# Modulation blocks one per tile in the gate and pointwise stages; the heads' token sums in an up-projection bank

## The chip, the cores and the metric

The kernel runs on one core of a Trainium2 chip. The metric is device time in microseconds from the start of the program to its end; the median of several runs is compared. The core has five engines that run side by side, each with its own instruction queue that is worked off strictly in order: TensorE (matrix products, PE in the profile, its weight loads PEld), VectorE (DVE), ScalarE (ACT), GpSimd (POOL) and SyncE (SP), which here issues every DMA. SBUF is the on-chip memory, PSUM the eight banks into which TensorE writes.

## What is computed

Two layers of a decoder trunk on 512 tokens of width 2048, in float32. Cut to what matters here:

```python
for l in range(2):
    mod = silu(c) @ ada_w[l] + ada_b[l]                 # (2048) @ (2048, 6144)
    shift, scale, gate = split(mod, 3)
    h = rms_norm(x, norm_g[l]) * (1 + scale) + shift
    z = h @ w_in[l]
    q_lat, kv_lat, k_rope, mla_gate, conv_in, conv_gate = split(z)
    # group B: 8 heads of latent attention, q and k RMS-normed per head (sums of squares per token)
    mla_out = attention(q_lat, kv_lat, k_rope) * silu(mla_gate)
    # group A: GLU, causal depthwise convolution (31 taps), LayerNorm, swish, pointwise product
    u = silu(layer_norm(conv31(glu(conv_in)))) @ w_pw[l] + b_pw[l]
    conv_out = u * silu(conv_gate)
    x = x + gate * (concat(mla_out, conv_out) @ w_out[l])
```

## The kernel before

Everything stands with channels on the 128 partitions and the 512 tokens along the row, so a tile is 128 x 512. Each large product runs in three passes (`mm3`, L248): weights and activations are split into a rounded part (hi) and a rest (lo), and hi x hi, hi x lo and lo x hi are added up in one PSUM bank. A weight chunk of 8 x 128 x 128 (512 KB) is loaded into one of four `raw` buffers by SP (`load_w`, L228), copied to hi by ScalarE (L242) and its rest taken by GpSimd, or by VectorE in layer 1's pointwise and output products (L243). `Stream` (L253) puts these steps in order: one step is four chunks of 128 channels, twelve matmuls.

The order on each queue is laid down when the program is built, by a planner that takes the instructions in the order of the source and lets a later one go first where its inputs and buffers are free. `tc.issue_after(ins)` adds an edge: instructions inside it come after `ins` on the engine of `ins` in that order. It adds no wait on the chip, and it does not touch instructions on other engines.

The stages of a layer are: the input products; eight heads of attention (`attend`, L735), between which the remaining input products are filled in (`fill`); then the **gate stage** (L905 to L930: eight tiles `cg`, the products of the convolution gate), the **pointwise stage** (L953 to L963: eight tiles `pw`, product with `w_pw`) and the **output projection** (L970 to L1017: sixteen tiles `wo`, 48 matmuls each). Beside the gate stage runs the LayerNorm of the convolution's result, as pieces in a queue `bgq` with a cost each; `bg(VBUD)` after each step takes pieces out until 1.5 is spent: the last convolution taps (`conv_ops`), two empty pieces, `ln_mean`, eight `ln_center`, two empty, the token sums of `vacc`, two empty, the spread of the result (`rsqrt_bc`), eight `ln_silu`. Their results are split into `u2`, which the pointwise product reads. `cat_split` (L939) splits the sixteen tiles of the concatenation for the output projection.

The modulation is computed in **blocks**: `Gemv.block` (L332) loads 128 rows of `ada_w` transposed, 1 MiB, into one of two `ada` buffers (SP, L335), and VectorE multiplies it by silu(c) and sums along the row in one instruction (L336). The list `todo` holds 64 blocks: 16 gates of layer 0, 32 scales and shifts of layer 1, 16 gates of layer 1. `more(n)` (L910) takes n blocks, fractions adding up. In layer 0's trailing stages 34 of them are done, in layer 1's 16. Before the change all stand in the output projection: `rate` blocks per tile, 34.5/15 and 16.5/15, each behind the instruction `behind`, which is the last split of the concatenation for the first tile and then the residual L1013 of the tile before. L1013 adds gate times the tile to x; its result is stored by SP (L1014), and the x of a tile is loaded by SP (L977).

`token_sums` (L188) sums a tile over its channels for each token, by eight or so one- or two-column matmuls into a PSUM bank of tag `pz`. That tag has one bank (L104); the transposes of the probabilities (`turn`, L741), `token_bc` and `ln_mean` use it too. The tag `up` has two, used by `up_head`, `up_values` and `values` in the heads. In the heads the sums of the next head are taken in `between` (L857), after the transposes of block 1, from F, which GpSimd adds up (L689, L690); `factors` (L694) reads them on VectorE (L701, L702).

Of the kernel before, what the change touches and what calls it, by code (L numbers as in the profile page):

```python
# [13 lines left out]
ALU = mybir.AluOpType  # L14
AX = mybir.AxisListType

P = 128
# [33 lines left out]
def hybrid_trunk(ctx, tc, xT, c, pos, invf, vec, adaT, w_s, w_t, w_kr, w_q, w_kv, w_pw, w_o, outT):  # L51
    nc = tc.nc
    V, A, T = nc.vector, nc.scalar, nc.tensor
# [52 lines left out]
    def psum(tag, n):  # L106
        return pp.tile([P, S], F32, tag=tag, bufs=NB[tag], name=nm(n))
# [77 lines left out]
        if scaled:  # L185
            V.tensor_scalar(out=y, in0=y, scalar1=RSCALE, scalar2=None, op0=ALU.mult)

    def token_sums(sq, rhs=None):  # L188

        ps, nt = psum("pz", "st"), sq.shape[1] // P  # L190
        rhs = ones[0:sq.shape[0], 0:1] if rhs is None else rhs
        w = rhs.shape[1]
        for i in range(nt):
            T.matmul(out=ps[:, i * w:(i + 1) * w], lhsT=sq[:, i * P:(i + 1) * P], rhs=rhs, start=True, stop=True)
        return ps[:, 0:nt] if w == 1 else ps[:, 0:nt * w].rearrange("p (i w) -> p i w", w=w)
# [101 lines left out]
    def bg(budget):  # L297
        while bgq and budget > 0:
            cost, fn = bgq.pop(0)
            fn()  # L300
            budget -= cost
# [43 lines left out]
    def gate(l, j):  # L345
        return mods[l][:, 32 + j:33 + j]
# [41 lines left out]
    def layer(l, xs, rstd, rpsum):  # L388
# [192 lines left out]
        for n in range(6):  # L581
            z = first[n]
# [111 lines left out]
        def factors(hd, st):  # L694

            e = hd % 2
            pst = lp.tile([P, 3, NT, 2], F32, tag="pst", name=nm("pst"))
            ms_, y, t = (pst[:, q] for q in range(3))

            b2 = lambda a: a.unsqueeze(2)  # L700
            V.tensor_mul(out=ms_[:, :, 0:1], in0=st[:, :, e:e + 1], in1=b2(rlat2[:, 1]))  # L701
            V.tensor_mul(out=ms_[:, :, 1:2], in0=st[:, :, 1 - e:2 - e], in1=b2(rlat2[:, 0]))  # L702
            V.tensor_add(out=ms_[:, :, 0:1], in0=ms_[:, :, 0:1], in1=b2(krs))
            V.tensor_scalar(out=ms_, in0=ms_, scalar1=1.0 / QKD, scalar2=EPS, op0=ALU.mult, op1=ALU.add)
            rsqrt_small(ms_, y, t)
            sc = lp.tile([P, NT], F32, tag="sc", name=nm("sc"))
            V.scalar_tensor_tensor(out=sc, in0=y[:, :, 1], scalar=SCALE, in1=rlat[:, 0], op0=ALU.mult, op1=ALU.mult)

            kft = lp.tile([P, NT], F32, tag="kft", name=nm("kft"))
            V.tensor_mul(out=kft, in0=y[:, :, 0], in1=rlat[:, 1])  # L710
            nc.sync.dma_start(out=kfd[l * H + hd], in_=kft)
            kf = ap.tile([P, S], F32, tag="kf", bufs=2, name=nm("kf"))
            nc.sync.dma_start(out=kf, in_=kfd[l * H + hd].rearrange("t i -> (t i)").partition_broadcast(P))
            return kf.rearrange("p (t i) -> p i t", i=NT), sc
# [128 lines left out]
            A.copy(out=RK[p0:p0 + 64, 0], in_=kr[0:64])  # L843
            V.tensor_sub(out=RK[p0:p0 + 64, 1 + p0 // 64], in0=kr[0:64], in1=f(RK[0:64, 0]))
        fill(1)
        fac = factors(0, token_sums(F, halves))
        conv_ops(0)
        fill(FA)
        for hd in range(H):
            fill(FB)  # L850
            if hd < H - 1:
                nxt = up_head(hd + 1)
            fill(FC)
            F = nxt[3]() if hd < H - 1 else None
            nfac = []

            def between():  # L857
                if hd < H - 1:
                    nfac.extend(factors(hd + 1, token_sums(F, halves)))
            pt = attend(hd % 2, *cur[:3], *fac, between)  # L860
            if hd % 2 == 0:
                vv_ = up_values(hd // 2)
            else:
                fill(FE)
            values(hd, pt, *vv_)
            cur, fac = nxt, nfac
# [4 lines left out]
        bp = phase.enter_context(tc.tile_pool(name=f"bp{l}", bufs=1))  # L871
        use_tmp(bp, 2)
        mean, vacc, crs = ms("mean"), ms("vacc"), ms("crs")
        ctile = []

        def ln_mean():
            pm = psum("pz", "pm")
# [3 lines left out]
        def ln_center(j):  # L881
            if j % 2 == 0:
                t = bp.tile([P, 2, S], F32, tag="c", bufs=4, name=nm("c"))
                nc.sync.dma_start(out=t, in_=cd[j // 2])
                ctile.extend((t[:, 0], t[:, 1]))
            V.tensor_sub(out=ctile[j], in0=ctile[j], in1=mean)
            square_sum(vacc, ctile[j], j)

        def ln_silu(j):
            V.tensor_mul(out=ctile[j], in0=ctile[j], in1=crs)  # L890
            A.activation(out=ctile[j], in_=ctile[j], func=AF.Silu, scale=vt("lng", j), bias=vt("lnb", j))

        bgq.extend((1.6, lambda: None) for _ in range(LAG))
# [31 lines left out]
        for j in range(NCC):  # L925
            for _ in range(4):
                ws.step()
                bg(VBUD)
        bg(1e9)
        cg = [t[:, e] for t in cg for e in range(2)]  # L930
        u2 = []
# [23 lines left out]
        for j in range(NCC):  # L955
            ws.step()
            ws.step()
            if j < 6:

                t = bp.tile([P, 2, S], F32R, tag="c", bufs=4, name=nm("cat")) if j < 4 else None  # L960
                cat[j] = cat_split(mout[j], t)
        for j in (6, 7):
            cat[j] = cat_split(mout[j])  # L963

# [8 lines left out]
        for j in range(KC):  # L973
# [36 lines left out]
                t = tp[:, j % 2]  # L1010
            else:
                t = ms("x1")
            behind = V.scalar_tensor_tensor(out=t, in0=z, scalar=gate(l, j), in1=xr, op0=ALU.mult, op1=ALU.add)  # L1013
            nc.sync.dma_start(out=outT[j] if last else x1d[j], in_=t)  # L1014
            if not last:
                nxs.append(t)
# [85 lines left out]
```

## Time and profile before

| | us |
|---|---|
| median of three runs | 1679.31 |
| lowest, highest | 1675.61, 1680.39 |
| the profiled execution | 1681.96 |
| its span, first to last instruction | 1680.2 |

The profile shows one execution. A row of grouped instructions gives engine, operation, output and inputs, their count, busy time and mean duration; a window row gives the busy time of each engine in a stretch, the clock granted to TensorE (1.00 is 2.4 GHz, 0.50 is 1.2 GHz), the busy share of the sixteen DMA engines and what they moved; the chain of waits follows the work that ended last back through what released it.

### The profile page before, as it was taken

How to read it: one execution, taken by the hardware profiler on the slowest of the kernel's cores; microseconds unless marked ns; L12 is line 12 of the kernel's file. 1: busy time of each engine (PE TensorE's matmuls, PEld its weight loads, DVE VectorE, ACT ScalarE, POOL GpSimd, SP SyncE). 2: the span in 40 equal slices, each digit the busy share in tenths (PEclk: the TensorE clock that was granted, in tenths of full speed). 3: DMA queues.
4: the chain of work that ended last, by engine and by line, in shares of the span. 5: the costliest groups of instructions: out<-in, count | busy, mean ns of one | idle time of the engine just before them, and what ended most of it. 6: DMA issues, size and time to landing. Idle time of an engine off the chain costs nothing.

```text
span 1680.2 us, 20681 instructions
## 1 busy us (share of the span) xinstructions
PE 1587.6 (94%) x7350; PEld 1299.3 (77%) x7350; DVE 1211.6 (72%) x2008; ACT 687.5 (41%) x1284; POOL 640.5 (38%) x440
## 2 busy tenths in 40 slices
PE   4988999999999999998899899999999999999999
PEld 2766778887878888877678678888787878888888
DVE  8898897888899645665469856677887786555553
ACT  4222455554544345321223355544544443532221
POOL 3565633424233445554535546243343326200000
PEclk9999999999999999999999999999999999999999
DMA  8878323222232732797885633233223335337672
GB/s 299 281 282 290 132 86 97 68 84 82 76 108 84 238 100 89 254 331 268 307 293 181 267 97 104 72 98 97 75 71 97 105 128 181 93 110 253 237 261 88
DMA packets 82890, 271.53 MB, mean 162 GB/s; under 512 B 10721, under 2 KB 21729, under 8 KB 70241
## 3 DMA queue, kind: packets, MB, share of 16 engines
q1 hardware_dynamic: 82786, 270.20, 47.5%
q8 instruction: 58, 0.95, 0.2%
q14 instruction: 46, 0.38, 0.1%
HBM read 257.55 MB, written 12.62 MB: 161 GB/s over the span
## 4 chain that ended last, share of the span: by engine, by line
PE 55%; DVE 27%; DMA 6%; ACT 6%; issue 3%; POOL 1%; SPq 0%; POOLq 0%; DVEq 0%; ACTq 0%
DVE ada L336 7%; DVE cv L547 7%; PE wo L251 4%; PE z L251 4%; PE z L249 4%; PE z L250 4%; PE wo L249 4%; PE wo L250 4%; PE cg L251 3%; PE cg L249 3%; PE cg L250 3%; DMA ada<-in_adaT_dram 3%; DMA raw<-in_w_o_dram 3%; PE pw L250 2%; PE pw L251 2%
## 5 line engine op out<-in xcount | busy, mean ns | idle before, releaser
L243 POOL TENSOR_TENSOR lo<-raw,hi 128x512 fp32r<-128x512 f32 x380 | 575.6, 1530 | 690.1 <-ACT hi L242 680.9
L242 ACT CAST hi<-raw 128x512 fp32r<-128x512 f32 (+1 forms) x512 | 306.4, 612 | 559.3 <-PE wo L250 152.9
L547 DVE SCALAR_TENSOR_TENSOR cv<-u,lvec,cv 128x512 f32<-128x512 f32 x464 | 348.7, 751 | 7.2
L249 PE MATMUL z<-h,hi 128*128 128x512 f32 (+1 forms) x782 | 308.2, 399 | 17.0 <-ACT h L357 10.9
L251 PE MATMUL z<-h,lo 128*128 128x512 f32 (+1 forms) x782 | 308.7, 395 | 8.6 <-POOL lo L243 8.5
L250 PE MATMUL z<-h,hi 128*128 128x512 f32 (+1 forms) x782 | 307.2, 393 | 0.7 <-DVE h L358 0.7
L336 DVE CUSTOM_DVE_ANT_0 ada<-ada,cb,avec 128x2048 f32<-128x2048 f32 x96 | 251.2, 2618 | 27.3 <-DMA ada<-in_adaT_dram 27.3
L249 PE MATMUL wo<-cat,hi 128*128 128x512 f32 (+1 forms) x544 | 207.8, 382 | 11.0 <-ACT hi L242 10.9
L251 PE MATMUL wo<-cat,lo 128*128 128x512 f32 (+1 forms) x544 | 207.9, 382 | 4.2 <-POOL lo L243 3.8
L250 PE MATMUL wo<-cat,hi 128*128 128x512 f32 (+1 forms) x544 | 207.0, 381 | 0.0
L249 PEld LDWEIGHTS z<-h,hi 128*128 128x128 f32 x782 | 150.0, 193 | 49.2 <-ACT h L357 13.4
L251 PEld LDWEIGHTS z<-h,lo 128*128 128x128 f32 x782 | 149.9, 192 | 43.3 <-POOL lo L243 13.5
L250 PEld LDWEIGHTS z<-h,hi 128*128 128x128 f32 x782 | 149.8, 192 | 29.5 <-DVE h L358 1.8
L243 DVE TENSOR_TENSOR lo<-raw,hi 128x512 fp32r<-128x512 f32 (+1 forms) x132 | 85.5, 660 | 80.3 <-ACT hi L242 80.1
L249 PEld LDWEIGHTS wo<-cat,hi 128*128 128x128 f32 x544 | 103.8, 191 | 32.0 <-ACT hi L242 13.1
L251 PEld LDWEIGHTS wo<-cat,lo 128*128 128x128 f32 x544 | 103.6, 190 | 26.3 <-POOL lo L243 6.8
L250 PEld LDWEIGHTS wo<-cat,hi 128*128 128x128 f32 x544 | 103.8, 191 | 19.0
L249 PE MATMUL cg<-h,hi 128*128 128x512 f32 x256 | 101.0, 394 | 0.0
L251 PE MATMUL cg<-h,lo 128*128 128x512 f32 x256 | 99.8, 390 | 0.0
L250 PE MATMUL cg<-h,hi 128*128 128x512 f32 x256 | 99.8, 390 | 0.0
L780 ACT ACTIVATE pr<-pr,smx,sc 128x128 f32<-128x128 f32 (+1 forms) x64 | 41.9, 654 | 110.3 <-DVE smx L779 110.2
L251 PE MATMUL mg<-h,lo 128*128 128x512 f32 x192 | 76.3, 397 | 2.3 <-POOL lo L243 2.3
(265 smaller groups left out, 2469.4 us busy)
## 6 DMA issues: line engine op xcount, KB each, us to landing
ada<-in_adaT_dram SPq DMA_DIRECT2D x96, 1024.0 KB, 5.5
raw<-in_w_t_dram SPq DMA_DIRECT2D x120, 512.0 KB, 3.9
raw<-in_w_o_dram SPq DMA_DIRECT2D x64, 512.0 KB, 5.8
raw<-in_w_s_dram SPq DMA_DIRECT2D x32, 512.0 KB, 6.4
raw<-in_w_pw_dram SPq DMA_DIRECT2D x16, 512.0 KB, 3.6
raw<-in_w_q_dram SPq DMA_DIRECT2D x24, 256.0 KB, 2.7
x<-in_xT_dram SPq DMA_DIRECT2D x8, 512.0 KB, 7.3
kf<-kfd SPq DMA_DIRECT2D x16, 256.0 KB, 3.9
```

Of the source, the lines that this page charges most:

```text
L242: A.copy(out=hiv, in_=rawv)
L243: i = eng.tensor_tensor(out=lov, in0=rawv, in1=f(hiv), op=ALU.subtract)
L249: T.matmul(out=ps, lhsT=whi, rhs=mhi, start=start, stop=False)
L250: T.matmul(out=ps, lhsT=whi, rhs=mlo, start=False, stop=False)
L251: T.matmul(out=ps, lhsT=wlo, rhs=mhi, start=False, stop=stop)
L336: V.tensor_tensor_reduce(out=t, in0=t, in1=self.cb, scale=1.0, scalar=vv(l, "ada_b", b), op0=ALU.mult, op1=ALU.add, accum_out=mods[l][:, b ...
L547: V.scalar_tensor_tensor(out=box[-1], in0=u[:, k:k + S], scalar=w, in1=box[0], op0=ALU.mult, op1=ALU.add)
L780: A.activation(out=pr[:, :n], in_=pr[:, :n], func=AF.Exp, scale=scl, bias=nb, accum_out=sums)
```

## The change

`token_sums` gets the bank's tag as an argument, and the heads' sums (not the latents', the rope key's or the LayerNorm's) use `up` in place of `pz`. `more(1)` is called after each of the eight gate tiles, behind the last `ln_center` or `ln_silu` instruction on VectorE and only once there is one, and after each of the first six pointwise tiles, behind the last split of the concatenation so far. In the output projection `behind` stays the last split of the concatenation, and `rate` is worked out from the blocks that are left.

```diff
         if scaled:
             V.tensor_scalar(out=y, in0=y, scalar1=RSCALE, scalar2=None, op0=ALU.mult)
-    def token_sums(sq, rhs=None):
-
-        ps, nt = psum("pz", "st"), sq.shape[1] // P
+    def token_sums(sq, rhs=None, tag="pz"):
+
+        ps, nt = psum(tag, "st"), sq.shape[1] // P
         rhs = ones[0:sq.shape[0], 0:1] if rhs is None else rhs
         w = rhs.shape[1]
         for i in range(nt):
@@ -843,7 +843,7 @@
             A.copy(out=RK[p0:p0 + 64, 0], in_=kr[0:64])
             V.tensor_sub(out=RK[p0:p0 + 64, 1 + p0 // 64], in0=kr[0:64], in1=f(RK[0:64, 0]))
         fill(1)
-        fac = factors(0, token_sums(F, halves))
+        fac = factors(0, token_sums(F, halves, "up"))
         conv_ops(0)
         fill(FA)
         for hd in range(H):
@@ -856,7 +856,7 @@
             def between():
                 if hd < H - 1:
-                    nfac.extend(factors(hd + 1, token_sums(F, halves)))
+                    nfac.extend(factors(hd + 1, token_sums(F, halves, "up")))
             pt = attend(hd % 2, *cur[:3], *fac, between)
             if hd % 2 == 0:
                 vv_ = up_values(hd // 2)
@@ -871,7 +871,7 @@
         bp = phase.enter_context(tc.tile_pool(name=f"bp{l}", bufs=1))
         use_tmp(bp, 2)
         mean, vacc, crs = ms("mean"), ms("vacc"), ms("crs")
-        ctile = []
+        ctile, ln_ins = [], [None]
         def ln_mean():
             pm = psum("pz", "pm")
@@ -883,11 +883,11 @@
                 t = bp.tile([P, 2, S], F32, tag="c", bufs=4, name=nm("c"))
                 nc.sync.dma_start(out=t, in_=cd[j // 2])
                 ctile.extend((t[:, 0], t[:, 1]))
-            V.tensor_sub(out=ctile[j], in0=ctile[j], in1=mean)
+            ln_ins[0] = V.tensor_sub(out=ctile[j], in0=ctile[j], in1=mean)
             square_sum(vacc, ctile[j], j)
         def ln_silu(j):
-            V.tensor_mul(out=ctile[j], in0=ctile[j], in1=crs)
+            ln_ins[0] = V.tensor_mul(out=ctile[j], in0=ctile[j], in1=crs)
             A.activation(out=ctile[j], in_=ctile[j], func=AF.Silu, scale=vt("lng", j), bias=vt("lnb", j))
         bgq.extend((1.6, lambda: None) for _ in range(LAG))
@@ -926,6 +926,9 @@
             for _ in range(4):
                 ws.step()
                 bg(VBUD)
+            if ln_ins[0] is not None:
+                with tc.issue_after(ln_ins[0].ins):
+                    more(1)
         bg(1e9)
         cg = [t[:, e] for t in cg for e in range(2)]
         u2 = []
@@ -959,6 +962,8 @@
                 t = bp.tile([P, 2, S], F32R, tag="c", bufs=4, name=nm("cat")) if j < 4 else None
                 cat[j] = cat_split(mout[j], t)
+                with tc.issue_after(cat_ins[0].ins):
+                    more(1)
         for j in (6, 7):
             cat[j] = cat_split(mout[j])
@@ -1010,7 +1015,7 @@
                 t = tp[:, j % 2]
             else:
                 t = ms("x1")
-            behind = V.scalar_tensor_tensor(out=t, in0=z, scalar=gate(l, j), in1=xr, op0=ALU.mult, op1=ALU.add)
+            V.scalar_tensor_tensor(out=t, in0=z, scalar=gate(l, j), in1=xr, op0=ALU.mult, op1=ALU.add)
             nc.sync.dma_start(out=outT[j] if last else x1d[j], in_=t)
             if not last:
                 nxs.append(t)
```

## Rows read from the trace of the kernel before

**Rows 1.** The page, busy time (share of the span) and count by engine.
```profile
PE 1587.6 (94%) x7350; PEld 1299.3 (77%) x7350; DVE 1211.6 (72%) x2008; ACT 687.5 (41%) x1284; POOL 640.5 (38%) x440
```
**Rows 2.** Windows by stage: window, length, busy and count by engine, clock, DMA share, GB/s.
```profile
545.00:640.00 95.00, 94.83 (x424) 78.02 (x424) 52.91 (x79) 42.33 (x69) 40.09 (x30) 1.00 0.45 150
640.00:680.00 40.00, 40.00 (x178) 33.08 (x177) 20.42 (x21) 17.46 (x31) 25.76 (x19) 1.00 0.37 114
690.00:866.00 176.00, 160.86 (x673) 128.89 (x671) 105.92 (x94) 39.49 (x68) 88.64 (x52) 0.96 0.85 307
1514.00:1666.00 152.00, 152.00 (x675) 126.00 (x674) 80.36 (x100) 34.38 (x55) 0.00 (x0) 1.00 0.63 224
```
**Rows 3.** The tile `wo`, its residual lines: count, min/median/max ns, first and last start.
```profile
L1013 DVE SCALAR_TENSOR_TENSOR x<-wo,mod,xr x15: 740/750/752, 689.9 to 866.5; 128x512 f32<-128x512 f32 x15
L1013 DVE SCALAR_TENSOR_TENSOR xr<-wo,mod,xr x15: 750/750/752, 1513.2 to 1665.6; 128x512 f32<-128x512 f32 x15
```
**Rows 4.** Windows cut at layer 0's L1013, three of them.
```profile
743.90:759.90 16.00, 13.08 (x49) 9.99 (x48) 8.50 (x8) 2.91 (x5) 7.40 (x4) 0.89 0.86 306
...
799.20:818.00 18.80, 14.35 (x49) 10.58 (x48) 6.28 (x6) 2.91 (x5) 6.76 (x6) 0.82 0.91 347
...
828.90:841.30 12.40, 11.20 (x49) 8.94 (x49) 5.90 (x7) 2.92 (x5) 6.44 (x4) 1.00 0.97 350
```
**Rows 5.** The chain that ended last, layer 0's output projection: start, length, what.
```profile
788.95 0.82 DVE ada L336
...
791.33 0.33 SPq L335
791.75 5.59 DMA raw<-in_w_o_dram
...
811.31 0.43 PE wo L249
```
**Rows 6.** SP's queue in layer 0's output projection: start, length, instruction, output and input.
```profile
677.75 0.33 SPq L232 DMA_DIRECT2D raw<-in_w_o_dram  x1
...
715.45 4.29 SPq L335 DMA_DIRECT2D ada<-in_adaT_dram  x2
...
736.08 4.97 SPq L335 DMA_DIRECT2D ada<-in_adaT_dram  x2
...
777.79 0.57 SPq L232 DMA_DIRECT2D raw<-in_w_o_dram  x1
...
789.06 0.33 SPq L1014 DMA_DIRECT2D x1d<-x  x1
```
**Rows 7.** The tile `ada`: durations in ns, and time from issue to landing.
```profile
L336 DVE CUSTOM_DVE_ANT_0 ada<-ada,cb,avec x96: 2339/2346/3404, 23.7 to 1655.4; 128x2048 f32<-128x2048 f32 x96
...
DMA to landing us min/median/max: 4.8/5.5/12.2
```
**Rows 8.** VectorE in layer 0's gate stage, in order of time; idle before and releaser in brackets.
```profile
597.95 2.68 DVE L886 TENSOR_TENSOR c<-c,mean 128x512 f32<-128x512 f32 x4 [25.50 <-ACT mean L879]
...
607.56 4.28 DVE L370 TENSOR_TENSOR vacc<-vacc,sq 128x512 f32<-128x512 f32 x3
...
617.15 0.16 DVE L215 TENSOR_SCALAR sm<-st 128x4 f32<-128x4 f32 x1 [5.31 <-PE st L194]
...
626.99 5.06 DVE L890 TENSOR_TENSOR c<-c,crs 128x512 f32<-128x512 f32 x8 [6.70 <-ACT crs L222]
...
634.18 5.15 DVE L935 TENSOR_TENSOR u<-c,u 128x512 fp32r<-128x512 f32 x8 [2.13 <-ACT u L934]
```
**Rows 9.** TensorE's waits, heads of layer 0, then of layer 1: total, times, longest.
```profile
PE st L194 <- DVE pt L751: 5.2, 5, 1.9
...
PE st L194 <- DVE pt L751: 2.7, 4, 1.1
```
**Rows 10.** GpSimd in order of time, the last step of one head's F.
```profile
299.30 1.29 POOL L690 TENSOR_TENSOR F<-F,rsq 64x512 f32<-64x512 f32 x1
```
**Rows 11.** The chain that ended last, that head's token sums.
```profile
309.04 1.05 PE st L194 x8
```

## Prediction

> **What bounds the kernel now.** I read the page first. TensorE is busy for 94% of the span [rows 1], so time is won only where it starves or runs slow. The stage windows, next, say where. Layer 1's output projection (the `wo` loop) runs without an idle moment at clock 1.00. Layer 0's, the same arithmetic, shows 160.9 us busy in 176 at clock 0.96, with the DMA engines at 307 GB/s instead of 224 [rows 2]. The gate stage and the pointwise stage of layer 0 have full TensorE and only 150 and 114 GB/s [rows 2]. The residual line L1013 puts a number on it: from first to last of 15 tiles it takes 1665.6 - 1513.2 = 152.4 us in layer 1, 10.89 us a tile, and 866.5 - 689.9 = 176.6 us in layer 0, 12.61 a tile [rows 3]. The difference, **24.2 us**, is all that can be won there.
>
> The windows cut at L1013 show how it is lost: in lumps, tiles of 16.0 and 18.8 us, whose clock is 0.89 and 0.82 [rows 4]. The chain of waits names the loop [rows 5]: a modulation block on VectorE, held behind tile 8's L1013, ends; SP then issues the next block's load, which needed that buffer; only then does SP issue the `w_o` load behind it, 5.59 us to land. TensorE waits for that, and then its matmuls stand 0.43 us apart (the 1.2 GHz level), against 10.89/48 = 0.227 in layer 1. In SP's own order, six `w_o` loads are out by 677.75, four more than tile 0 needs; when tile 8's store goes out at 789.06 only twenty are, the last at 777.79: tile 9's own two and none ahead [rows 6]. So SP's in-order queue, filled with 1 MiB block loads, is the bound there; the bytes are the reason. A tile moves 1 MiB of weights and 0.25 + 0.25 MiB of x, 1.573 MB; 34 blocks over 15 tiles are 2.3 a tile, 2.38 MB more. At 10.89 us that is 363 GB/s; the best tile reaches 350 [rows 4].
>
> **Moved blocks, layer 0.** `more(1)` behind a gate tile runs only once `ln_ins` is set. Stepped through by hand, the queue enters the stage with 49 pieces of convolution at 0.6, three a step, so 17 steps; then two empty pieces, the mean in step 19, the centres from step 20, the last step of tile 4. The trace agrees: VectorE idles 25.5 us with the convolution done and starts the centres at 597.95, late in the stage [rows 8]. Tiles 4 to 7 thus give **4** blocks, not 8; the pointwise stage gives 6; 24 of 34 stay. Two are loaded before the `wo` loop in either kernel, so 22 loads (23.07 MB) fall into it instead of 32 (33.55 MB). At an even 24.5/15 = 1.63 a tile the demand would be (1.63 x 1.049 + 1.573)/10.89 = 302 GB/s, below the 307 it has now, and the whole 24.2 us would come back.
>
> But they won't be even. Without the edge to L1013 a block is bound only behind the last split of the concatenation, and runs as soon as it has landed. Two buffers then set the cadence: 5.5 us of landing, 2.35 of VectorE and 0.33 of issue, 8.2 us a pair [rows 6, 7]; six issues from 715.45 to 736.08 say 20.6/5 = 4.1 a block, the same [rows 6]. Eleven pairs take 90 us, 8.3 tiles at full pace, 2.65 a tile: **denser than before, for a shorter time**. In that front stretch 23.07 + 8.3 x 1.573 = 36.1 MB must come. TensorE covers 8.3 tiles and, by the loads ahead, about one more (an estimate from rows 6): 9.3 x 10.89 = 101.3 us. At the 307 GB/s that the loop has on average the bytes take 117.7, 16.4 too long; at 350, the best tile, 103.2, 1.9 too long. The same sum for before (55.6 MB over 14 tiles at 307: 181 against 163) gives 18 us where 24.2 is measured, so I scale by 1.34 for the matmuls at 0.43: a loss of 22 or 2.5. I take the middle rate, 328: 110.1 - 101.3 = 8.8, times 1.34 = 11.8, so a gain of **12.4**, ends 2.2 and 21.7 (24.2 if even). The middle, since the loop of rows 5 loses one of its links (the block no longer waits for L1013), while the store L1014 still holds SP until TensorE is done.
>
> **Cost where the blocks go, layer 0.** Each is 2.35 us, 3.40 beside GpSimd [rows 7]. In the pointwise stage VectorE has 19.6 us idle of 40 [rows 2]; six blocks are 14 to 20 us. They can delay a PSUM read by at most 3.4 us, and four banks hold 21 us of tiles there: nothing, and if that cover were gone, 3.4 us. Their loads stand in SP's queue ahead of `w_pw` loads: 6.3 MB over 40 us adds 157 GB/s to 114, still under 307. In the gate stage the first block goes between centre 1 and centre 2 and the second behind centre 7. The LayerNorm chain has slack: `vacc` ends at 611.8 and is read at 617.15 after an idle 5.3 us, then VectorE idles 6.7 us before L890 [rows 8]. Two blocks (4.7 to 6.8 us) about fill the first slack; up to 1.5 us could reach TensorE. The third fits the second. The fourth sits behind `ln_silu(5)`, ahead of 6 and 7, at 631 us: ScalarE's Silu of 6 waits 1.6 to 2.7 us, and `u2` is only just in time now, its subtraction starting at 634.18 [rows 8]. From 0 to 4.2 in all; I take **+1.8**, near the low end, as TensorE needs chunk 6 only 4 us into the stage.
>
> **Layer 1.** Eleven of its 16 blocks move likewise (5 and 6; there the centres start in tile 3). Its `wo` loop has no idle to win [rows 2]; its pointwise stage also carries the weight splits on VectorE, and two blocks in the way would cost 0 to 2 us. I take 0, keeping -1 (224 GB/s falls) to +2.
>
> **Token sums in an `up` bank.** Now the single `pz` bank must be cleared by the probabilities' split L751 first. TensorE waits for that 5.2 us (5 times) in layer 0 and 2.7 (4 times) in layer 1 [rows 9]. The sums' input is ready long before: for one head GpSimd ends F at 300.6, the sums start at 309.04 [rows 10, 11]. So the wait goes; what comes next, the scores and a filling step, is ready. The `up` banks are read long before this point, and the next user, `vz` or `pv`, finds the other bank free; it could wait behind VectorE's queue of taps, which I bound by the 2.7 us that the sums themselves lose to VectorE in layer 1 now. From -7.9 to +2.7; I take **-6**, nearer the row. TensorE's saving there carries on: in layer 0 the last convolution is done 25.5 us before its mean is asked for [rows 8].
>
> **Sum:** -12.4 + 1.8 + 0 - 6 = **-16.6 us**. Against the profiled execution's 1681.96 (span 1680.2 and 1.8 around it) that is 1665.4; this execution lies 2.65 above the median of the runs, so for the median 1679.31 - 16.6 = **1662.7**.
>
> **Rivals.**
> *Full relief.* SP's order interleaves the blocks so that `w_o` keeps its lead: -24.2 - 7.9 + 0 = 1647. For it: the freed DMA time and the missing link. Against: nothing spaces the blocks now. The Trainium skill (DMA: Bandwidth & Descriptors, Specifications) puts the HBM limit of one core at about 358 GB/s; the best row, 350 [rows 4], agrees nearly. By it the 36.1 MB would take 100.8 us, within the 101.3, and this rival would come true.
> *Eaten by the front.* The stretch runs at the old mean of 307: -2.2 + 1.8 - 6 = -6.4, **1673**. For it: the queue is no shorter per block, and SP's waits for buffers and stores remain.
> *Slower.* SP's order packs three blocks a tile in front. 22 blocks are then 7.3 tiles, two of them covered by the lead; if each of the other 5.3 costs what a starved tile costs now (16.0 and 18.8 against 10.89, +6.5 [rows 4]) the loop loses 34.5, 10.3 more than now: +10.3 + 1.8 - 6 = +6.1, **1685**. It decides from a loss of 33.4 on (24.2 + 6 - 1.8 + 5). Against it: even now only every other tile starves.
> *Not what it says.* If the sums in the new bank wait as long as before, 6 us are missing: 1669. Rows 10 and 11 speak against it.
>
> **How the numbers follow.** A measurement of this kernel tells about 0.3%, 5 us, from no change. My forecast has 0.42 (the missing-sums case within it), full relief 0.20, eaten by the front 0.23, slower 0.13, and 0.02 for anything else. Faster by over 5 us (under 1674.3): 0.42 + 0.20 + half of the third, 0.12 = 0.74. Within: 0.11 + 0.03 = 0.14. Slower: 0.12. The range goes from full relief to the weak end of the third with the late fourth block and nothing from the sums (1673 + 2.4 + 6): 1647 to 1682.
>
> **What would show it.** L1013's 15 of layer 0 spanning some 164 us instead of 176.6, with starved tiles only among the first nine and the blocks done near tile 9; four block instructions between 598 and 640 and six from there to the first `wo` tile; gate and pointwise windows above 200 GB/s at full TensorE; no wait of the sums on L751, about 6 us less in the two attention stages; `pw` starting no more than 3 us later relative to the last `cg`. Wrong, if the blocks still run to the last tile, if `w_o` loads in SP's queue fall behind earlier than now, or if `pw` waits on `u2` for over 4 us.

## The result, and the profile after

| | before | after |
|---|---|---|
| median, us (five runs each, side by side) | 1680.39 | 1668.02 |
| lowest, highest | 1675.61, 1683.13 | 1662.6, 1670.4 |
| span of the profiled execution | 1680.2 | 1666.2 |

The changed kernel takes 0.9919 of the time before, 95% interval 0.9895 to 0.9943: 12.4 us less by the medians, 14.0 by the spans of the two profiled executions. Forecast were 1662.7 us and 16.6 us less. Nearly the same sum came about from quite different terms.

A table of stage lengths shows that best. Each boundary is the first matmul of the stage's tile; the output projection is cut at the residual line, L1013 before and L1018 now (line numbers behind L926 have grown by three to five), and the first column of the pair is layer 0:

| us | before, layer 0 / 1 | after, layer 0 / 1 | difference |
|---|---|---|---|
| heads (first sums of kv to first `cg`) | 331.5 / 368.6 | 324.6 / 365.1 | -6.9 / -3.5 |
| gate stage (first `cg` to first `pw`) | 91.6 / 93.3 | 99.2 / 100.7 | +7.6 / +7.4 |
| pointwise stage (first `pw` to first `wo`) | 44.0 / 43.6 | 44.1 / 43.5 | 0.1 / -0.1 |
| first `wo` tile, to its residual | 11.5 / 11.0 | 19.2 / 11.1 | +7.7 / +0.1 |
| 14 tiles, first to 15th residual | 176.6 / 152.4 | 150.6 / 152.3 | -26.0 / -0.1 |

TensorE's share of the span went from 94% [rows 1] to 95%.

Windows by stage, of after, answering to [rows 2]: window, its length, busy time and count of PE, PEld, DVE, ACT and POOL, granted clock, DMA share, GB/s. The last two lines are cuts of 5 us out of layer 0's gate stage.

```profile
540.00:635.00 95.00, 90.65 (x391) 74.24 (x389) 56.46 (x76) 37.01 (x59) 44.08 (x29) 0.96 0.53 181
635.00:675.00 40.00, 39.86 (x176) 33.03 (x177) 37.31 (x34) 17.07 (x32) 28.86 (x15) 1.00 0.61 219
698.00:848.00 150.00, 150.00 (x664) 124.20 (x663) 82.93 (x74) 42.18 (x69) 94.11 (x52) 1.00 0.85 301
610.00:615.00 5.00, 1.95 (x9) 1.95 (x10) 3.20 (x5) 0.00 (x0) 4.12 (x2) 0.83 0.87 332
615.00:620.00 5.00, 5.00 (x13) 3.84 (x13) 1.96 (x9) 0.28 (x1) 0.00 (x0) 0.50 0.56 213
```

Layer 0's output projection (third line) now has a full TensorE at clock 1.00 with 301 GB/s; before it was 160.86 us busy in 176 at 0.96 with 307. The gate stage (first line) was full and is not: 90.65 of 95, clock 0.96. The residual line, of after, against [rows 3] (count, min/median/max ns, first and last start):

```profile
L1018 DVE SCALAR_TENSOR_TENSOR x<-wo,mod,xr x15: 739/750/752, 697.8 to 848.4; 128x512 f32<-128x512 f32 x15
L1018 DVE SCALAR_TENSOR_TENSOR xr<-wo,mod,xr x15: 747/751/752, 1499.3 to 1651.6; 128x512 f32<-128x512 f32 x15
```

Layer 0 takes 848.4 - 697.8 = 150.6 us for its 14 intervals, even less than layer 1's 152.3. That needs a caution. The first residual is late, and part of the work of the tiles behind it was done before it. The measure used below is therefore the **loop sum**, first tile and 14 tiles together: 188.1 us before, 169.8 after, 163.4 in layer 1 of both. So the loop had 24.7 us to win, and won 18.3.

TensorE's waits over the whole span, of after, against [rows 9] (the waiting tile, what released it, total us, times, longest):

```profile
PE st L194 <- DVE vacc L370: 8.5, 2, 4.2
...
PE pz L746 <- DVE pt L751: 5.7, 6, 1.7
```

The sums' wait on the probabilities' split, 5.2 + 2.7 us before, is gone. But the transposes of the probabilities (`pz`), which keep that bank, now wait for the split 5.7 us, against 1.3 before; *The sums alone* returns to this. New are two waits of the sums of `vacc`, one in each layer, and two of the first `wo` tile on the last splits of the concatenation, 1.97 and 1.04 us. No `wo` matmul waits for weights any more.

**The gate stage.** VectorE in order of time, of after, against [rows 8] (start, length, instruction, idle before and releaser in brackets):

```profile
590.42 1.47 DVE L886 TENSOR_TENSOR c<-c,mean 128x512 f32<-128x512 f32 x2 [25.49 <-ACT mean L879]
591.82 2.34 DVE L336 CUSTOM_DVE_ANT_0 ada<-ada,cb,avec 128x2048 f32<-128x2048 f32 x1
...
603.99 2.34 DVE L336 CUSTOM_DVE_ANT_0 ada<-ada,cb,avec 128x2048 f32<-128x2048 f32 x1
...
607.96 3.37 DVE L336 CUSTOM_DVE_ANT_0 ada<-ada,cb,avec 128x2048 f32<-128x2048 f32 x1
...
611.26 1.74 DVE L370 TENSOR_TENSOR vacc<-vacc,sq 128x512 f32<-128x512 f32 x1
...
671.51 3.38 DVE L336 CUSTOM_DVE_ANT_0 ada<-ada,cb,avec 128x2048 f32<-128x2048 f32 x1
...
677.46 3.38 DVE L336 CUSTOM_DVE_ANT_0 ada<-ada,cb,avec 128x2048 f32<-128x2048 f32 x1
...
685.73 2.35 DVE L945 TENSOR_TENSOR cat<-part,cat 128x512 fp32r<-128x512 f32 x2
```

Three blocks stand between the first centre and the last addition into `vacc`. Before, that chain ran from 597.95 to about 611.8, 13.9 us; now from 590.42 to 613.0, 22.6 us, though it starts earlier. The difference is the three blocks, 2.34 + 2.34 + 3.37 = 8.05 us, and little else. TensorE, of after, at both places where it pays (start, length, matmul, idle before in brackets):

```profile
613.05 1.68 PE L194 MATMUL st<-ones,vacc 128*128 128x1 f32 x8 [4.25 <-DVE vacc L370]
...
615.59 0.63 PE L251 MATMUL cg<-h,lo 128*128 128x512 f32 x1
616.01 0.63 PE L249 MATMUL cg<-h,hi 128*128 128x512 f32 x1
...
682.41 0.39 PE L251 MATMUL wo<-cat,lo 128*128 128x512 f32 x1
684.77 0.65 PE L249 MATMUL wo<-cat,hi 128*128 128x512 f32 x1 [1.97 <-ACT cat L944]
686.46 0.80 PE L250 MATMUL wo<-cat,hi 128*128 128x512 f32 x1 [1.04 <-DVE cat L945]
```

The same sums in the kernel before, without a wait:

```profile
616.17 0.95 PE L194 MATMUL st<-ones,vacc 128*128 128x1 f32 x8
```

Here the price of these stalls can be read. TensorE, ahead of which many `cg` matmuls were ready, stood 4.25 us because the sums come first in its queue. Then the matmuls of 615.59 and 616.01 start 0.43 us apart, and 13 of them go at that pace, from 614.59 to 620.21, in 5.62 us instead of 13 x 0.227 = 2.95. The window 615 to 620 says the same: a granted clock of 0.50, the 1.2 GHz level, behind one of 0.83 with the stall in it. From the sums to the next matmul it takes 1.54 us; before, where that matmul started at 616.98, it took 0.81, 0.73 less. Idle 4.25, slow 2.67 and these 0.73 make 7.65, all of the stage's +7.6. In the first `wo` tile two waits of 1.97 and 1.04 us leave twelve matmuls between 684.77 and 691.72 at the slow pace: from 682.64, where the next should have started, 9.08 us instead of 12 x 0.227 = 2.72. That is 6.4 us, and 169.8 - 163.4 = 6.4 us is all that the loop still loses.

### The profile page after: what moved, and what is told of

Same layout as the page of the kernel before. It is cut to its first block, busy times and chain, and to the rows that moved or that the text cites. A ratio compares the mean times of both kernels' runs of the same rounds, so it can differ in the third digit from the quotient of the medians.

```text
span 1666.2 us, 20654 instructions
## 1 busy us (share of the span) xinstructions
PE 1581.1 (95%) x7350; PEld 1300.9 (78%) x7350; DVE 1226.2 (74%) x2008; ACT 687.4 (41%) x1284; POOL 659.7 (40%) x440
## 4 chain that ended last, share of the span: by engine, by line
PE 62%; DVE 28%; ACT 6%; issue 3%; DMA 1%; POOL 1%; SPq 0%; POOLq 0%; ACTq 0%; DVEq 0%
DVE ada L336 7%; PE wo L250 7%; PE wo L251 7%; PE wo L249 7%; DVE cv L547 5%; PE z L249 4%; PE z L251 4%; PE z L250 4%; PE cg L249 3%; PE cg L251 3%; PE cg L250 3%; PE mg L251 2%; PE mg L249 2%; PE mg L250 2%; DVE x L356 2%
## 5 line engine op out<-in xcount | busy, mean ns | idle before, releaser
L243 POOL TENSOR_TENSOR lo<-raw,hi 128x512 fp32r<-128x512 f32 x380 | 595.2, 1581 | 657.5 <-ACT hi L242 647.3
L336 DVE CUSTOM_DVE_ANT_0 ada<-ada,cb,avec 128x2048 f32<-128x2048 f32 x96 | 257.4, 2682 | 40.5 <-DMA ada<-in_adaT_dram 40.4
L249 PE MATMUL cg<-h,hi 128*128 128x512 f32 x256 | 103.0, 402 | 0.0
L250 PE MATMUL cg<-h,hi 128*128 128x512 f32 x256 | 101.5, 397 | 0.0
L357 ACT ACTIVATE h<-x,mod 128x512 fp32r<-128x512 f32 (+1 forms) x34 | 23.3, 697 | 136.8 <-DVE mod L336 100.5
```

The costliest lines, as they stand in the source:

```text
L243: i = eng.tensor_tensor(out=lov, in0=rawv, in1=f(hiv), op=ALU.subtract)
L249: T.matmul(out=ps, lhsT=whi, rhs=mhi, start=start, stop=False)
L250: T.matmul(out=ps, lhsT=whi, rhs=mlo, start=False, stop=False)
L336: V.tensor_tensor_reduce(out=t, in0=t, in1=self.cb, scale=1.0, scalar=vv(l, "ada_b", b), op0=ALU.mult, op1=ALU.add, accum_out=mods[l][:, b ...
L357: A.activation(out=hi, in_=x, func=AF.Identity, bias=shift(l, j))
```

## The experiments

Theory A, formed from the two traces: the loop recovers because ten blocks fewer are loaded in it; the gate stages lose 7.5 us each because blocks run ahead of `vacc`'s chain; the first tile loses about 6 because the last two pointwise blocks run ahead of the last splits; the heads gain 10. Its rivals were the other readings of each: that the freedom from L1013 wins the loop, that two buffers or SP's order were the bound and not the bytes, that the sums win little.

After was timed beside a before of 1680.39 only. The runs below have their own before beside them, 1681.62 to 1682.06, and the ratios go by that; "under after" compares with 1668.02 all the same and can be off by some 2 us, as the medians of before differ by 1.7.

### The sums alone

Before, with `token_sums` in an `up` bank in the heads and nothing else.

```diff
-                    nfac.extend(factors(hd + 1, token_sums(F, halves)))
+                    nfac.extend(factors(hd + 1, token_sums(F, halves, "up")))
```

> The kernel before with only the heads' token sums in an up bank. Theory (each part of the change acts for itself; the two attention stages gained some 10 us in the changed kernel through the freed wait): both attention stages together 8 to 11 us shorter, everything behind them unchanged, gate stages of 92 us from first cg to first pw matmul, L1013 of layer 0 still spanning 174 to 179 us; in all 8 to 11 us under the kernel before. Rival (the transposes of the probabilities now wait in place of the sums, and most of the 10 us came from a reshuffled order elsewhere): 0 to 4 us under it.

Measured: 1669.02 us against 1682.06, ratio 0.9932 (0.9913 to 0.9951). The span is 11.3 us under that of before. The heads take 324.7 and 365.1 us (-6.8 and -3.5), every other stage of the table is as before but for some 3 us of the `wo` loop, whose loop sum is 185.1 against 188.1. Nothing was changed in that loop, so 3 us of a starved loop's sum come and go without an edit to it. This edit alone is worth more than all the rest of the change as it stands.

The heads gain 10.3 us, where the listed wait was 7.9. Windows over the heads of layer 0 and of layer 1, of before and then of this kernel, say what kind of time it was:

```profile
211.30:542.80 331.50, 319.52 (x1567) 264.82 (x1568) 286.18 (x638) 179.50 (x364) 116.63 (x90) 0.98 0.28 85
996.70:1365.30 368.60, 359.45 (x1753) 297.29 (x1752) 278.56 (x619) 185.18 (x371) 137.22 (x106) 0.99 0.29 88
```
```profile
210.70:535.40 324.70, 314.33 (x1567) 262.86 (x1568) 289.17 (x638) 179.07 (x364) 116.77 (x90) 0.99 0.29 86
988.90:1354.00 365.10, 357.32 (x1753) 297.89 (x1752) 277.26 (x619) 185.07 (x371) 136.85 (x106) 0.99 0.29 88
```

TensorE's idle time fell from 21.13 to 18.15 us only, 3.0 less. The transposes' waits, of before and then of this kernel, say why: as the rival had it, they now wait in place of the sums.

```profile
PE pz L746 <- DVE pt L751: 1.3, 2, 0.7
```
```profile
PE pz L746 <- DVE pt L751: 5.8, 6, 1.7
...
PE pz L746 <- DVE pst L186: 2.7, 3, 2.0
...
PE pz L746 <- DVE kft L710: 1.4, 1, 1.4
```

The other 7.3 us is busy time: the same 1567 and 1753 matmuls took 679.0 us before and take 671.7 now. One wait of before and one of this kernel, each with a window behind it:

```profile
388.25 1.60 PE L194 MATMUL st<-halves,F 128*128 128x2 f32 x8 [1.91 <-DVE pt L751]
390.00:395.00 5.00, 5.00 (x14) 3.93 (x14) 3.56 (x14) 1.92 (x4) 0.31 (x1) 0.50 0.00 0
```
```profile
392.81 0.63 PE L746 MATMUL pz<-ident,pr 128*128 128x128 f32 x4 [2.03 <-DVE pst L186]
393.00:398.00 5.00, 5.00 (x29) 4.25 (x27) 4.79 (x12) 1.84 (x4) 0.00 (x0) 1.00 0.52 111
```

Behind the wait in front of the sums the clock is 0.50, behind the wait in front of the transposes 1.00. In before, 27 matmuls of 512 columns behind three of the sums' waits go at the slow pace; here none does behind a wait of the transposes. At 0.43 against 0.227 us that is 5.5 of the 7.3 us. The length of a wait doesn't decide it: 1.18 us in an earlier head (309.04) left eight slow matmuls in before, 1.19 in the same place none in *The moved blocks alone*, and the 2.03 us that leave none here are 2.07 in *Both* and leave five. What decides it is not shown. The gain is steady all the same: the heads of both layers take 698.5 to 700.1 us in the four profiles with the sums in `pz`, and 689.5 to 692.8 in the eight with them in `up`.

### The moved blocks alone

After, with the sums back in the `pz` bank and with blocks in the loop again behind L1018.

```diff
-                    nfac.extend(factors(hd + 1, token_sums(F, halves, "up")))
+                    nfac.extend(factors(hd + 1, token_sums(F, halves)))
...
-            V.scalar_tensor_tensor(out=t, in0=z, scalar=gate(l, j), in1=xr, op0=ALU.mult, op1=ALU.add)
+            behind = V.scalar_tensor_tensor(out=t, in0=z, scalar=gate(l, j), in1=xr, op0=ALU.mult, op1=ALU.add)
```

> The kernel before with the blocks moved one per tile into the gate and pointwise stages, the remaining ones still held behind the residual L1013 tile by tile, sums in pz. Theory A (fewer blocks in the output projection are what wins): L1013 of layer 0 spans 150 to 158 us instead of 176.6; gate stages still some 7 us longer each and the first output tile some 8 us late, so in all 0 to 8 us under the kernel before. Theory B (freeing the blocks from L1013 is what wins): L1013 spans over 165 us, and in all the kernel is 5 to 15 us slower than before.

The residual line of this kernel, columns as above:

```profile
L1018 DVE SCALAR_TENSOR_TENSOR x<-wo,mod,xr x15: 750/751/752, 704.8 to 857.1; 128x512 f32<-128x512 f32 x15
```

857.1 - 704.8 = 152.3 us: full pace, with the blocks bound as before. The loop sum is 170.0, as in after. Yet the kernel takes 1680.25 us, ratio 0.9988 (0.9975 to 1.0): the gate stages lose 7.6 and 7.1, and its TensorE waits 4.3 us for `vacc` in each layer. The move wins 18 us in one place and pays 15 in two others.

### The unbinding alone

Before, with `behind = ` dropped at L1013.

```diff
-            behind = V.scalar_tensor_tensor(out=t, in0=z, scalar=gate(l, j), in1=xr, op0=ALU.mult, op1=ALU.add)
+            V.scalar_tensor_tensor(out=t, in0=z, scalar=gate(l, j), in1=xr, op0=ALU.mult, op1=ALU.add)
```

> The kernel before with only this edit: in the output projection the blocks are all held behind the last split of the concatenation, none moved, sums in pz. Theory A (fewer blocks win): 34 blocks remain, L1013 of layer 0 spans 168 to 185 us, in all within 8 us of the kernel before. Theory B (freeing wins): L1013 spans 150 to 158 us and the kernel is 18 to 25 us under the kernel before, with nothing lost in the gate stages.

The residual line, then a line of TensorE's waits from 660 to 860:

```profile
L1013 DVE SCALAR_TENSOR_TENSOR x<-wo,mod,xr x15: 740/747/752, 692.9 to 861.5; 128x512 f32<-128x512 f32 x15
```
```profile
PE wo L249 <- ACT hi L242: 11.3, 4, 4.1
```

1683.42 us, ratio 1.0012 (0.9997 to 1.0028): no difference. The 14 tiles take 168.6, but the first takes 16.3, and the loop sum is 184.9 against 188.1. TensorE still waits 11.3 us for weights. Freeing the blocks from L1013 without having fewer of them does next to nothing: its 3.2 us are about what the loop of *The sums alone* won without an edit.

### The gate blocks behind the last addition

After, with the place in VectorE's order at which gate blocks may stand moved from the first centre to the last addition into `vacc`, which `square_sum` now returns.

```diff
-            ln_ins[0] = V.tensor_sub(out=ctile[j], in0=ctile[j], in1=mean)
-            square_sum(vacc, ctile[j], j)
+            V.tensor_sub(out=ctile[j], in0=ctile[j], in1=mean)
+            add = square_sum(vacc, ctile[j], j)
+            if j == NCC - 1:
+                ln_ins[0] = add
```

> The changed kernel, with the gate stage's blocks held behind the last addition into vacc (one block fewer in each gate stage, it goes to the output projection). Theory (the blocks between the centres delay vacc, TensorE stands 4.2 us at the sums of vacc and then runs at 1.2 GHz for some 13 matmuls): no wait of the sums on vacc, both gate stages back to 91 to 94 us from first cg to first pw matmul, in all 12 to 15 us under the changed kernel, near 1654. Rival (the block loads in SP's queue make the gate stage's weights late, the wait on vacc being hidden behind it): the gate stages stay at 97 to 100 us, within 4 us of the changed kernel.

VectorE in order of time, of this kernel:

```profile
591.83 2.68 DVE L886 TENSOR_TENSOR c<-c,mean 128x512 f32<-128x512 f32 x4 [25.48 <-ACT mean L879]
...
601.44 4.27 DVE L370 TENSOR_TENSOR vacc<-vacc,sq 128x512 f32<-128x512 f32 x3
605.64 3.38 DVE L336 CUSTOM_DVE_ANT_0 ada<-ada,cb,avec 128x2048 f32<-128x2048 f32 x1
```

1654.85 us, ratio 0.9849 (0.9829 to 0.9868), 13.2 us under after. Gate stages 91.5 and 93.3, as before the change; the chain now takes 13.9 us, from 591.83 to 605.7, and two blocks follow it. The wait for `vacc` is gone. The waits of the first tile on the splits stay, 2.0 and 1.2 us, and so does the loop sum, 169.9.

### Four pointwise blocks in place of six

After, with `more(1)` only in the first four pointwise tiles.

```diff
-                with tc.issue_after(cat_ins[0].ins):
-                    more(1)
+                if j < 4:
+                    with tc.issue_after(cat_ins[0].ins):
+                        more(1)
```

> The changed kernel with pointwise blocks only behind the first four tiles' splits (two fewer, they go to the output projection). Theory (the blocks late in the pointwise stage, 3.4 us each beside GpSimd, push the last splits of the concatenation past the sixth chunk of the first output tile, where TensorE waits 3 us and then runs at 1.2 GHz): no wait of wo on a split over 0.5 us in layer 0, first wo matmul to first L1018 11 to 14 us instead of 19.2, in all 4 to 7 us under the changed kernel. Rival (the first output tile is late for the two blocks that run in front of its L1018, as many as before): that stretch stays at 17 to 20 us and the total within 2 us of the changed kernel.

1664.0 us against 1681.88, ratio 0.9895 (0.987 to 0.992), 4.0 under after. The waits on the splits are gone and the loop sum is 163.4, layer 1's. The bracket for the first tile was missed, 15.8 us: the residual alone is late there, since two blocks stand ahead of it on VectorE, and the 14 tiles are shorter for it, 147.6. TensorE loses nothing. Since the loop won 6.4 us and the total 4.0, some was given back: this profile's heads are 3 us longer than after's. TensorE waits 2.71 us there for VectorE, at 236.56, a wait that after's profile doesn't have.

### Both

The gate blocks behind the last addition, and four in the pointwise stage.

> Both edits: gate blocks behind the last addition into vacc, pointwise blocks behind the first four tiles only. In layer 0 seven blocks are moved instead of ten. Theory (the two losses are separate): gate stages 91 to 94 us, first stretch 11 to 14, L1018 of layer 0 spanning 149 to 154, in all 17 to 20 us under the changed kernel, near 1649. Rival (27 blocks are again too many for the output projection): L1018 spans over 158 us and the total is no better than 1655.

The window over the 14 tiles of this kernel, columns as above, and TensorE's only wait from 590 to 840:

```profile
689.00:837.00 148.00, 148.00 (x655) 122.55 (x654) 92.73 (x82) 40.94 (x69) 95.59 (x51) 1.00 0.90 326
```
```profile
PE pw L250 <- DVE u L940: 0.2, 1, 0.2
```

1648.96 us, ratio 0.9808 (0.9786 to 0.983), 19.1 under after. Loop sum 163.4 with 27 blocks in it, at clock 1.00 and 326 GB/s. (First tile 15.5 and 14 tiles 147.9 miss their brackets by the same shift as above.)

### Two more blocks, ahead of the mean

As the last, with a block in place of each of the two empty pieces that precede the mean, where VectorE idles 25 us; they may stand behind the last convolution tap.

```diff
-        bgq.extend((1.6, lambda: None) for _ in range(LAG))
+        def early_block():
+            with tc.issue_after(csum_ins[0].ins):
+                more(1)
+        bgq.extend((1.6, early_block) for _ in range(LAG))
```

> As the kernel with both edits, and one block in place of each of the two empty queue pieces ahead of the mean, held behind the convolution's last addition, where VectorE has stood idle for 25 us: two more blocks moved in each layer. Theory (idle VectorE time off the LayerNorm chain takes blocks for nothing): gate stages stay at 91 to 94 us and the total is 0 to 3 us under the kernel with both edits. Rival (the additional block loads in SP's queue hold back weight loads): gate stages 95 us or more, total above it.

1649.04 us, ratio 0.9805 (0.9783 to 0.9827). Gate stages 91.5 and 93.4, so blocks ahead of the mean cost nothing; but the loop sum was already full, 163.4 again, and there is nothing left to win with two loads fewer.

### Three buffers

Before, with three `ada` buffers in place of two.

```diff
-    GB, GC = 2, 15
+    GB, GC = 3, 15
```

> The kernel before with three buffers for the modulation blocks instead of two. It has the same bytes in the same stages. Theory (SP's in-order queue is the bound of layer 0's output projection: it stands at a block load until a buffer is free, and w_o loads stand behind): L1013 of layer 0 spans 155 to 168 us instead of 176.6, in all 8 to 20 us under the kernel before. Rival (363 GB/s asked for where the best tile moved 350: the bytes are the bound): L1013 spans 172 us or more and the total is within 5 us.

SP's largest waits from 690 to 866, of the kernel before, then of this one, then, from 690 to 850, of after (what waits, what released it, total us, times, longest):

```profile
SPq L335 <- DVE mod L336: 77.3, 28, 5.4
SPq L1014 <- DVE x L1013: 51.0, 14, 10.6
```
```profile
SPq L1014 <- DVE x L1013: 75.9, 14, 9.7
SPq L335 <- DVE mod L336: 51.9, 23, 5.9
```
```profile
SPq L232 <- POOL lo L243: 48.2, 23, 5.0
SPq L1019 <- DVE x L1018: 46.1, 13, 5.7
SPq L335 <- DVE mod L336: 21.7, 10, 4.3
```

1677.48 us, ratio 0.997 (0.9957 to 0.9983); 14 tiles in 171.2, loop sum 182.7 against 188.1. The expectations of both theories for the 14 tiles are missed, the buffers' at its upper end and the bytes' by under 1 us; the total, 4.4 us under before, is the rival's. A third buffer wins 5.4 of the loop's 24.7 us, of which 3.0 are within what such a loop differs by. But SP stands as long as before: 25 us went from its wait for a block's buffer (77.3 to 51.9) to its wait at the store (51.0 to 75.9). So this run doesn't tell what a queue that waits less would be worth, and the bytes are not separated from the places in the queue. The third fence is how a cured loop looks: SP now waits most for a free weight buffer, that is, the `w_o` loads are as far ahead as four `raw` buffers let them be.

### Both, with the blocks bound

As *Both*, with blocks behind the residual again.

```diff
-            V.scalar_tensor_tensor(out=t, in0=z, scalar=gate(l, j), in1=xr, op0=ALU.mult, op1=ALU.add)
+            behind = V.scalar_tensor_tensor(out=t, in0=z, scalar=gate(l, j), in1=xr, op0=ALU.mult, op1=ALU.add)
```

> The kernel with both edits (gate blocks behind the last addition into vacc, pointwise blocks behind the first four tiles), its remaining blocks of the output projection again held behind the residual of the tile before. Theory (how many blocks are left in that loop decides, not what they are held behind): first wo matmul of layer 0 to last residual line 162 to 167 us, as the 163.4 with both edits, total within 4 us of that kernel. Rival (27 blocks need the freedom): over 172 us, total 8 us or more above it.

Its residual line:

```profile
L1021 DVE SCALAR_TENSOR_TENSOR x<-wo,mod,xr x15: 750/751/752, 684.7 to 837.0; 128x512 f32<-128x512 f32 x15
```

1648.07 us, ratio 0.9799 (0.9783 to 0.9814). First tile 11.1 and 14 tiles 152.3: the same 163.4 us, with no shift of the residual. So the third edit of the change, the unbinding, is worth nothing, with many blocks (above) or with fewer. This is the version to keep: 20 us under after, and it can't be told from *Both*.

### Three blocks moved

As *The gate blocks behind the last addition*, with none in the pointwise stage: 31 of 34 stay in the loop.

```diff
-                with tc.issue_after(cat_ins[0].ins):
-                    more(1)
```

> The changed kernel with gate blocks behind the last addition into vacc and no blocks at all in the pointwise stage: three moved in layer 0, 31 of 34 left in the output projection, unbound. By the bytes a tile then asks for (31/15 x 1.049 + 1.573)/10.89 = 343 GB/s, next to the 350 of the best tile. Theory (bytes): first wo matmul to last residual between the 184.9 of 34 unbound blocks and the 163.4 of 27, 170 to 181 us, total 1655 to 1666. Rival (a few blocks less suffice once they are unbound): 163 to 167 us, total near 1650.

The window over the loop, and the largest of TensorE's waits in it:

```profile
675.00:842.00 167.00, 164.56 (x724) 133.96 (x723) 113.52 (x98) 43.28 (x75) 95.29 (x56) 1.00 0.88 319
```
```profile
PE wo L251 <- POOL lo L243: 2.0, 5, 0.9
```

1652.98 us, ratio 0.9825 (0.9803 to 0.9848). Loop sum 168.6, between the brackets of the two theories. With 34, 31 and 27 unbound blocks the loop takes 184.9, 168.6 and 163.4. Three blocks take off 16.3 us, of which their own bytes, 3.15 MB at 319 GB/s, would be 9.9 (an estimate); the next four find only 5.2 left to win. Each is one profile.

## Why the prediction came out as it did

**What bounds the loop: right as far as the runs go.** Fewer block loads cure it (*The moved blocks alone*, *Both*, *Three blocks moved*), freedom from L1013 does not, and a third buffer helps little. That "the bytes are the reason" is argued, not shown: every run that has fewer bytes also has fewer loads in SP's queue. For the bytes speaks that 363 and 343 GB/s were asked for with 34 and 31 blocks, and that 326 is the most that a loop with a full TensorE moved.

**The loop's gain: right mechanism, the term mis-sized.** Forecast -12.4, measured -18.3, and -24.7 once the first tile is left alone. The step that failed is "denser than before, for a shorter time", 2.65 blocks a tile from a cadence of 4.1 us. I had taken that cadence from blocks that follow each other as fast as two buffers let them, and left the `w_o` loads between them out. In after, the 24 blocks of the loop start between 688.01 and 818.98 us, 5.7 us apart, about two a tile over twelve tiles, where I had expected them done near tile 9. The trace shows what spaces them. SP in order of time, one tile of after:

```profile
719.48 0.44 SPq L335 DMA_DIRECT2D ada<-in_adaT_dram  x1
720.02 3.28 SPq L232 DMA_DIRECT2D raw<-in_w_o_dram  x2
723.40 0.38 SPq L335 DMA_DIRECT2D ada<-in_adaT_dram  x1
729.50 0.33 SPq L1019 DMA_DIRECT2D x1d<-x  x1
```

A block's load stands behind `w_o` loads that wait for their buffers, 48.2 us in 23 waits, and behind the store, which waits for the residual, 46.1 in 13 (the third fence of *Three buffers*). In this in-order queue the weights and the stores pace the blocks, once the weights are ahead; "nothing spaces the blocks now" was the error. *Full relief* was thus the right rival for the loop, and *eaten by the front* and *slower* fell: no tile starves. The rate of transfer that I took, 328 GB/s, was about right: *Three blocks moved* holds 319 and *Both* 326. The Trainium skill (DMA: Bandwidth & Descriptors, Specifications) gives about 358 GB/s as the HBM limit of a core; no run here shows it held, and 326 over 148 us with a full TensorE is the most that one does.

**The gate stage, layer 0: wrong.** Forecast +1.8 (0 to 4.2), measured +7.6. Two steps failed. The first is the third block, "The third fits the second" slack. The other two ran where I had put them, between centres 1 and 2 at 591.82 and behind centre 7 at 603.99. But `issue_after` is a lower bound on the place. The third, bound behind centre 7 as well, was put at 607.96, still ahead of `vacc`'s last addition. The second is the slack itself. I read 5.3 us, VectorE's idle time up to L215; but what reads `vacc` are the sums on TensorE, and they started at 616.17, 4.3 us behind the end of the last addition at 611.84. The chain grew by 22.6 - 13.9 = 8.7 us, and 8.7 - 4.3 = 4.4, against a wait of 4.25. And I priced a stall at its length, though [rows 5] had shown that matmuls stand 0.43 us apart behind one; here 2.67 us more. With *The gate blocks behind the last addition* both gate stages are back at their length, and the total is 13.2 us under after.

**The gate stage, layer 1: wrong.** Forecast 0 (-1 to +2), measured +7.4, by the same wait of 4.2 us. I weighed only its output and pointwise stages there, and never asked for the slack of its LayerNorm chain, though I had for layer 0. It is the costliest gap of the working, since one view would have filled it.

**The pointwise stage: the stage right, its end missed.** "Nothing" holds for the stage (44.0 to 44.1 us). But the last two blocks, at 671.51 and 677.46, took 3.38 us each beside GpSimd, and pushed the splits of tiles 6 and 7 of the concatenation from 680.9 to 685.73; the first `wo` tile needs them from 682.4 on. I looked at the `pw` reads, for which four banks are cover, and not at who reads the splits. The cover of 3.4 us that I named was a bound for one late read, and the price was 6.4. For the 3.38 us: the Trainium skill (SBUF — State Buffer, Who interferes with whom) states that a VectorE instruction with two SBUF inputs contends with a GpSimd instruction that reads SBUF; the rows agree, 2.34 to 2.35 us for all sixteen blocks of layer 1 before, beside an idle GpSimd, and 3.38 for these two, with GpSimd at work during them.

**The heads: the sign right, the working only in part.** Forecast -6 (-7.9 to +2.7), measured -10.4, and -10.3 in *The sums alone*, outside my range. The step that failed is "So the wait goes". The 7.9 us of listed waits went from the sums, but the transposes wait instead, and TensorE's idle time fell by 3.0 only. The larger part, 7.3 us, is that the same matmuls take less time, mostly those behind the sums' waits, which ran at 0.43. My sum had no term for that, though [rows 5] shows the pace behind a wait.

**The sum.** Against the forecast the loop won 5.9 us more and the heads 4.4 more, the gate stages lost 5.8 and 7.4 more, and the rest is 0.3: -16.6 became -14.0. The time was held by errors that cancelled, not by the working.

## What to carry to other kernels

Low-priority work put into an engine's idle time must stand behind the end of any chain whose slack is smaller than the work: read that chain to its last reader in every layer and at both ends of the stage, and tie the work to the last instruction of the chain instead of the first. Price a stall of TensorE by the matmuls behind it and not by its length alone: here some stalls cost nearly twice their length or more, and others no more than it. In an in-order DMA queue, look at all its waits together: 25 us less at one of them were 25 more at the next.

## What the runs showed of the hardware

- A stall can cost more than its length: 4.25 us of idle left 13 matmuls at 0.43 us apart, +2.67 us; waits of 1.97 and 1.04 us in the first `wo` tile left twelve, and cost 6.4 in all. It need not: 2.03 us in front of the transposes left the clock at 1.00, where 1.91 in front of the token sums left it at 0.50. The same wait went either way in different executions.
- With TensorE full at clock 1.00 the DMA engines held 326 GB/s for 148 us. The 307 GB/s of the starved loop before was no ceiling.
- The loop's time against its blocks has a knee: 34, 31 and 27 blocks take 184.9, 168.6 and 163.4 us, the last the pace of layer 1's loop, in which TensorE never stands.
